# Hybrid block on one core: the hand-over from the mixer to the feed forward with its steps on VectorE in another order

## Chip, core and metric

The kernel runs on one core of a Trainium2 chip. The metric is the device time of one execution in microseconds (us). All tensors are float32. The five engines of the core each run their own queue of instructions in order: TensorE (PE: matmuls, with weight loads shown as PEld), VectorE (DVE), ScalarE (ACT), GpSimd (POOL) and SyncE (SP, which here only issues loads). They wait for each other through semaphores.

## What is computed

The reference is one block of a network on 512 tokens of 1024 features. The part that matters here, cut down:

```python
    # h, conv_out, ssm_out: norm, one large projection, a convolution branch and a state-space branch
    mixed = (g_conv * conv_out + g_ssm * ssm_out) @ w_out[i]
    x = x + rms_norm(mixed, mix_post_g[i])
    h = rms_norm(x, ffn_pre_g[i])
    gt, up = jnp.split(h @ w_gate_up[i], 2, axis=-1)       # 2 x 2816 columns
    f = (jax.nn.silu(gt) * up) @ w_down[i]
    x = x + rms_norm(f, ffn_post_g[i])
```

The hand-over is everything between the product with `w_out` and the product with `w_gate_up`: a norm, a residual sum, a second norm, and the transposition of `h` into the form in which the feed forward multiplies it.

## The kernel before

Each float32 product is made of three matmuls in a reduced form: an operand is split into a high part (a cast on ScalarE) and a low part (source minus high part), and `mm3` (L184 to L189) adds high x high, low x high and high x low. The low part is a subtraction on VectorE, or, for some weights, the negated high part written by ScalarE to which a load issued from POOL adds the weight from memory: an **adding load** (`accum_op=ALU.add`). `halve` (L927) makes the parts of a gate/up block, and `ADD_LO` (L78) names the units whose first block gets its low part by an adding load.

**Token tiles.** The product with `w_out` is made for four tiles of 128 tokens, t = 0 to 3, in `tm_step`. After each, `residual(t)` (L991) norms the result: the squares are summed on ScalarE (`mean_sq`), VectorE multiplies by the gain (`mg`, L1000), `factor` adds the two halves of the sum on VectorE (`pm`, L873) and raises them to -1/2 on POOL (`rs`, L874), VectorE adds the scaled result to x (`xr`, L1006). A second `mean_sq` and `factor` (`rs_b`) follow, and VectorE writes the diagonal matrix `dg` (L1010). `transposed(t)` (L1014) multiplies `xr` by `dg` on PE, which transposes and scales at once (tile `ptr`, L1023); the two halves of the result are scaled by the gain of the second norm into `xg`, the first half on VectorE (L1030), the second in four pieces on ScalarE (L1035).

**Halves.** The feed forward multiplies by Winograd's form of Strassen's scheme: seven products of halves instead of eight. The moving operands are b11 and b21 (from tiles 0 and 2), b22 and the sums t1 to t4 (from all tiles); for the second half of the tokens they are complete only after tile 3. `sums` and `rest` make them (L1060, L1066), each in a high and a low part.

**Units.** The 5632 columns of `w_gate_up` are cut into 22 units of 256, u = 0 to 21, gate and up in turn. A unit has two raw blocks of 128 x 1024 with the parts a11, a12 and a21, a22. `prep_a` makes the forms of a11 and a12; `prep_s` (L949) makes the sums s1 to s4 on VectorE (L956 to L961) and their forms (tiles `whi_g`/`wlo_g`, `chi_g`/`clo_g`, `dhi`/`dlo`, all at L930 and L935). A unit's seven products, 12 matmuls of 256 columns each, have names in the code:

- `first(u)`: a11 b11 into X and a12 b21 into Y, in one bank for the first four units;
- `begin(u)`: ScalarE copies X (L1118) and VectorE adds Y (L1107); this has to be done before X is used again;
- `x2(u)`: s2 t2 added into X; `v1(u)`: s1 t1; `x3(u)`: s3 t3; `v2(u)`: s4 b22; `x4(u)`: a22 t4 into X. After x2, v1 and x3 ScalarE or VectorE take the result over before the next product adds to the same bank.

The first four units overlap the hand-over in an order written out by hand. Before tile 3 is transposed PE makes `first(0)`, `first(1)`, `first(2)`; after it `first(3)` and then

```python
    start = {0: "v0 x0 v1 w0 y0", 1: "x1 w1 z0 y1", 2: "x2 v2 z1 y2", 3: "x3 v3 z2 w2 y3"}
    step = {"v": v1, "x": x2, "w": v2, "y": x3, "z": x4}
```

where the figure is the unit. From unit 4 on a loop makes them in a regular order.

The order of the instructions on an engine is decided before the run: the framework places each one by its estimate and by the order of the program's text, and `not_before` (L179) adds an order without a wait on data. `hold` is a pair of instructions: while it is set, forms and sums of weights are not placed ahead of them on ScalarE and VectorE. Raw blocks are loaded from SP into five shared buffers (`w_raw`, L142), so a load waits until the block that held its buffer has been split.

Of the kernel before, what the change touches and what calls it, by code (L numbers as in the profile page):

```python
# [10 lines left out]
F32 = mybir.dt.float32  # L11
# [66 lines left out]
ADD_LO = (2, 3) + tuple(range(7, FF // P, 2))  # L78
# [46 lines left out]
def block_kernel(ctx: ExitStack, tc: tile.TileContext, x, xT, x0, prm, hp, gp, w, out):  # L125
# [743 lines left out]
    def factor(ss, tag):  # L869

        rs = sm.tile([P, 1], F32, tag="rs1", bufs=2, name=f"rs_{tag}")
        m = sm.tile([P, 1], F32, tag="pm1", bufs=2, name=f"pm_{tag}")
        mark["pm"] = dve.tensor_scalar(out=m, in0=ss[0], scalar1=ss[1], scalar2=RMS_EPS, op0=ALU.add, op1=ALU.add)  # L873
        pool.tensor_tensor(out=rs, in0=m, in1=neg_half[:, :1], op=ALU.pow)  # L874
        return rs
# [72 lines left out]

    def prep_s(u):  # L949

        if u >= NF or (u, "s1") in forms:
            return
        ra, rb_ = g_raw(u, 0), g_raw(u, 1)
        (a11, a12), (a21, a22) = [(r[:, :T], r[:, T:]) for r in (ra, rb_)]
        s1_ = w2.tile([P, T], F32, tag="s1", bufs=2, name=f"s1_{u}")
        sum_ = dve.tensor_tensor(out=s1_, in0=a21, in1=a22, op=ALU.add)  # L956
        if hold:
            not_before(sum_, hold[1])
        dve.tensor_tensor(out=a21, in0=a11, in1=a21, op=ALU.add)
        dve.tensor_tensor(out=a11, in0=s1_, in1=a11, op=ALU.add)  # L960
        dve.tensor_tensor(out=a12, in0=a11, in1=a12, op=ALU.add)  # L961

        def s1_halves():
            halve(("s1",), u, s1_, [w2.tile([P, T], F32R, tag=tg, bufs=2, name=f"{tg}_{u}") for tg in ("dhi", "dlo")])

        def halves():
            halve(("s2", "s4"), u, ra, pair_of_tiles())
            if u != 1:
                s1_halves()
            halve(("s3", "a22"), u, rb_, pair_of_tiles())  # L970

        if u == 1:
            s1_halves()
        if u > 1:
            halves()
        return halves
# [14 lines left out]
    def residual(t, ps):  # L991
# [6 lines left out]
        for n, c in enumerate(cols2):  # L998
            ss.append(mean_sq(ps[n], pbp, f"a{t}", n))
            m = dve.tensor_tensor(out=mg[:, c], in0=ps[n], in1=gpost0[:, c], op=ALU.mult)  # L1000
        if t == 3:
            hold += [mark["sq"], m]
        rs = factor(ss, f"a{t}")
        ss = []
        for n, c in enumerate(cols2):
            dve.scalar_tensor_tensor(out=xr[:, c], in0=mg[:, c], scalar=rs, in1=xr[:, c], op0=ALU.mult, op1=ALU.add)  # L1006
            ss.append(mean_sq(xr[:, c], pbp, f"b{t}", n))
        rs = factor(ss, f"b{t}")
# [5 lines left out]
    def transposed(t):  # L1014
# [4 lines left out]
        for n in range(2):  # L1019
# [9 lines left out]
            if n == 0:  # L1029
                dve.tensor_tensor(  # L1030
# [49 lines left out]
    for t, k in steps:  # L1080
        (mh, ml), tok = mt[t // 2], slice(t % 2 * P, (t % 2 + 1) * P)
        tm_step(ps, t, k, NK, mh[:, k, tok], ml[:, k, tok], split[wo0 + k])
        if k == NK - 1:
            residual(t, ps[t])
            if t == 2:
                others()
# [5 lines left out]
        if (t, k) == (2, 5):  # L1092
            sums, others = transposed(1)
            sums()
        if (t, k) in ((3, 1), (3, 2)):
            prep_a(k + 1)
        if (t, k) == (3, 4):
# [13 lines left out]
    def begin(u):  # L1111

        f, e = u // 2, u % 2
        if e == 0:
# [19 lines left out]
    hold[1] = mark["pm"]  # L1134
    mark["chain"] = True
    for u in range(3):
        first(u)
        if u == 0:
            halves = prep_s(1)
# [3 lines left out]
    more_raw.append(h2e)  # L1143
    begin(0)
    sums()
    rest()
    hold[:] = mark["t3"]
# [11 lines left out]

    def x2(u):  # L1160
# [5 lines left out]
    def v1(u):  # L1166
        if u < EARLY_U:
            V[u] = bank(f"v{u}")[:, :HB]
        product(V[u], u, "s1", "t1", True)
        act.copy((D_[u][1] if u in D_ else begin(u)[1])[:, c2], V[u])  # L1170

    def x3(u):
        f, e = u // 2, u % 2
        d = D_[u][1][:, c2]
# [4 lines left out]
        else:  # L1179
            gated_by(d, d, sg[f][1][:, c2])  # L1180

    def v2(u):
# [6 lines left out]
        else:  # L1189
            dve.tensor_tensor(out=d, in0=d, in1=sg[f][0], op=ALU.mult)  # L1190

    def x4(u):
# [5 lines left out]
        else:  # L1198
            gated_by(d, X[u], sg[f][1][:, c1])
# [301 lines left out]
```

## Time and profile before

| | before |
|---|---|
| runs | 1029.85, 1036.62, 1037.15 us; median 1036.62 |
| profiled execution | 1036.17 us, of which the span is 1034.4 us |
| PE busy | 1024.2 us (99%), granted clock 0.998 on average |
| VectorE busy | 814.3 us (79%) |
| ScalarE busy | 609.0 us (59%) |
| POOL busy | 96.4 us (9%) |
| memory traffic | 150.82 MB, mean 146 GB/s |

In a row of the timeline stand the start and the duration in us, the engine, the line, the operation, the output and the inputs by their names in the program, the shape, and in brackets the idle time of the engine just before with what ended it. All times count from the start of the span. Token tile 3 leaves PE near 698 us, its transposition stands at 706.6, and unit 4 begins at 738.9.

### The profile page before, as it was taken

The page shows a single profiled execution, that of the slowest core. Times are in us where ns is not written, and L with a number is a line of the kernel's source. Part 1 is how long each engine was busy: PE and PEld are TensorE (multiplying, and loading weights), DVE is VectorE, ACT ScalarE, POOL GpSimd, SP SyncE. Part 2 cuts the span into 40 slices and gives each one's busy share as a digit, 9 for nine tenths or more (in the row PEclk, how much of TensorE's full clock was granted, in tenths as well). Part 3 has the DMA queues.
Part 4 walks back from the last instruction along what each step waited for, and adds up shares of the span by engine and source line. Part 5 has one row for each costly group of instructions (what it writes and reads, how often), then busy time and mean ns, then how long its engine had stood idle before and what let it go on. Part 6 is the DMA issues. An engine that isn't in the chain of part 4 may idle for free.

```text
span 1034.4 us, 15686 instructions
## 1 busy us (share of the span) xinstructions
PE 1024.2 (99%) x6089; PEld 890.9 (86%) x6089; DVE 814.3 (79%) x1184; ACT 609.0 (59%) x1032; POOL 96.4 (9%) x122
## 2 busy tenths in 40 slices
PE   9999999999999999999999999999999999999997
PEld 7898889888888888888888888889999999998885
DVE  7899976959594979398976455579997788799874
ACT  7655776575748464844532673366665565568552
POOL 0101101110111011101100000010000000001000
PEclk9999999999999999999999999999999999999999
DMA  8567634655546454644452223433565345469622
GB/s 298 156 164 213 165 81 140 184 157 148 135 131 163 124 157 128 163 122 122 110 133 84 82 85 99 183 105 121 167 184 157 105 143 146 123 197 278 214 82 82
DMA packets 42458, 150.82 MB, mean 146 GB/s; under 512 B 4880, under 2 KB 5904, under 8 KB 41360
## 3 DMA queue, kind: packets, MB, share of 16 engines
q1 hardware_dynamic: 30672, 104.66, 29.9%
q0 software_dynamic: 9504, 38.80, 19.0%
q10 hardware_dynamic: 2208, 6.36, 1.8%
q8 instruction: 48, 0.79, 0.3%
q14 instruction: 26, 0.21, 0.1%
HBM read 145.54 MB, written 4.26 MB: 145 GB/s over the span
## 4 chain that ended last, share of the span: by engine, by line
PE 93%; DVE 3%; ACT 2%; issue 1%; DMA 0%; POOL 0%; SPq 0%; ACTq 0%; POOLq 0%; DVEq 0%
PE xy L187 4%; PE xy L186 4%; PE xy L188 4%; PE pz L187 3%; PE pz L188 3%; PE pz L186 3%; PE pso L186 3%; PE pso L187 3%; PE pso L188 3%; PE px L188 3%; PE px L187 3%; PE px L186 3%; PE yv L187 2%; PE yv L188 2%; PE yv L186 2%; PE yd L636 2%
## 5 line engine op out<-in xcount | busy, mean ns | idle before, releaser
L152 ACT CAST whi<-raw 128x1024 fp32r<-128x1024 f32 (+2 forms) x116 | 115.0, 1003 | 157.3 <-PE pso L187 37.5
L444 DVE SCALAR_TENSOR_TENSOR a<-v,prm_t,a 128x511 f32<-128x511 f32 (+15 forms) x240 | 179.8, 752 | 16.1 <-ACT a L441 13.8
L158 DVE TENSOR_TENSOR wlo<-raw,whi 128x1024 fp32r<-128x1024 f32 (+2 forms) x76 | 85.8, 1134 | 42.8 <-ACT whi L152 42.1
L156 POOL DMA_DIRECT2D wlo<-in_w x40 | 35.7, 893 | 353.5 <-ACT wlo L155 120.9
L188 PE MATMUL pz<-whi,hlo 128*128 128x512 f32 (+2 forms) x160 | 56.3, 352 | 0.0
L187 PE MATMUL pz<-wlo,hhi 128*128 128x512 f32 (+2 forms) x160 | 56.1, 351 | 0.0
L186 PE MATMUL pz<-whi,hhi 128*128 128x512 f32 (+2 forms) x160 | 55.4, 353 | 0.0
L186 PE MATMUL px<-hhi,whi 128*128 128x512 f32 x128 | 50.2, 392 | 0.0
L186 PE MATMUL pso<-yh,whi 128*128 128x512 f32 x128 | 50.0, 393 | 0.0
L188 PE MATMUL px<-hhi,wlo 128*128 128x512 f32 x128 | 49.8, 389 | 0.0
L187 PE MATMUL px<-hlo,whi 128*128 128x512 f32 x128 | 49.8, 389 | 0.0
L187 PE MATMUL pso<-yl,whi 128*128 128x512 f32 x128 | 49.7, 390 | 0.0
L188 PE MATMUL pso<-yh,wlo 128*128 128x512 f32 x128 | 49.7, 389 | 0.0
L930 ACT CAST whi_g<-raw 128x1024 fp32r<-128x1024 f32 x40 | 41.3, 1053 | 13.7 <-PE yv L187 8.6
L528 DVE SCALAR_TENSOR_TENSOR x<-px,prm_t,x 128x511 f32<-128x511 f32 (+2 forms) x48 | 34.7, 741 | 13.8 <-ACT x L526 13.8
L935 DVE TENSOR_TENSOR wlo_g<-raw,whi_g 128x1024 fp32r<-128x1024 f32 x34 | 41.1, 1218 | 5.1 <-ACT whi_g L930 4.7
L155 ACT ACTIVATE wlo<-whi 128x1024 fp32r<-128x1024 f32 x40 | 42.2, 1055 | 0.3
L426 ACT ACTIVATE L<-L,nacs 128x128 f32<-128x128 f32 x128 | 38.8, 389 | 0.5 <-POOL L L419 0.4
L186 PEld LDWEIGHTS pz<-whi,hhi 128*128 128x128 f32 x160 | 30.2, 189 | 3.9
L187 PEld LDWEIGHTS pz<-wlo,hhi 128*128 128x128 f32 x160 | 30.2, 188 | 3.8
L188 PEld LDWEIGHTS pz<-whi,hlo 128*128 128x128 f32 x160 | 30.1, 188 | 3.7
L930 ACT CAST chi_g<-raw 128x1024 fp32r<-128x1024 f32 x24 | 24.8, 1050 | 11.4 <-PE yv L187 5.1
(656 smaller groups left out, 3344.8 us busy)
## 6 DMA issues: line engine op xcount, KB each, us to landing
raw<-in_w SPq DMA_DIRECT2D x186, 512.0 KB, 4.5
wlo<-in_w POOLq DMA_DIRECT2D x40, 512.0 KB, 6.8
L<-scr POOLq DMA_DIRECT2D x8, 1024.0 KB, 7.1
wlo_g<-in_w POOLq DMA_DIRECT2D x11, 512.0 KB, 7.1
clo_g<-in_w POOLq DMA_DIRECT2D x7, 512.0 KB, 5.3
xr<-in_x ACTq DMA_DIRECT2D x4, 512.0 KB, 4.7
x2d<-xr ACTq DMA_DIRECT2D x4, 512.0 KB, 2.9
xres<-x2d SPq DMA_DIRECT2D x4, 512.0 KB, 3.7
```

The costliest lines, as they stand in the source:

```text
L152: act.copy(hi[:, c], src[:, c])
L155: act.activation(lo[:, c], hi[:, c].bitcast(F32), AF.Copy, scale=-1.0)
L156: mark["lo"] = pool.dma_start(lo[:, c], w[n][:, c].bitcast(F32R), accum_op=ALU.add)
L158: mark["wlo"] = dve.tensor_tensor(out=lo[:, c], in0=src[:, c], in1=hi[:, c].bitcast(F32), op=ALU.subtract)
L186: mark["pe"] = pe.matmul(ps, lh, rh, start=start, stop=False, skip_group_check=more)
L187: pe.matmul(ps, lh, rl, start=False, stop=False, skip_group_check=more)
L188: mark["pe3"] = pe.matmul(ps, ll, rh, start=False, stop=stop, skip_group_check=more)
L426: act.activation(L[:, h, c, :], L[:, h, c, :], AF.Exp, bias=nacs[:, c, HG * g + h : HG * g + h + 1])
L444: return dve.scalar_tensor_tensor(out=va[j][:, d:], in0=vs[j][:, : T - d], scalar=col("dw_w", j * KC + KC - 1 - d), in1=va[j][:, d:], op0= ...
L528: dve.scalar_tensor_tensor(out=a[:, d:], in0=ps[:, : T - d], scalar=col("ssm_w", i * KS + KS - 1 - d), in1=a[:, d:], op0=ALU.mult, op1=ALU ...
L930: a_ = act.copy(hi, src)
L935: d_ = dve.tensor_tensor(out=lo, in0=src, in1=hi.bitcast(F32), op=ALU.subtract)
```

## The change

1. `transposed(2)` scales both halves of the third tile on VectorE.
2. `hold` now ends, for the last tile, with the residual sum `xr` instead of `mg`; for unit 0 it is moved on to `dg` while its blocks are split, and it is set to `pm` later.
3. For unit 1 the block sum s1 = a21 + a22 is made by loads: `load_s1` brings a21 from SP, `add_s1` adds a22 from POOL, placed not before the power of the third tile. a21 + a11 is then rebuilt as a difference.
4. `ADD_LO` names unit 4 too: the low part of its a11 and a12 comes by an adding load.
5. The `sums` of tile 1 and of tile 3 are called at other places, `begin(1)` is called before the splitting of unit 1, and gets a tile `d1` of its own in place of half of `f32`, which does not exist yet at that point. Its results go to `f32` through `f_out`.
6. For units 2 and on, the first block sum of `prep_s` is held behind t4.

```diff
@@ -75,7 +75,7 @@
 EARLY_U = 4
 DMA_EVERY = 2
 DMA_FROM = 8
-ADD_LO = (2, 3) + tuple(range(7, FF // P, 2))
+ADD_LO = (2, 3, 4) + tuple(range(7, FF // P, 2))
 GU_AHEAD = 5
 MOV_AT = 192
 S_AHEAD = 5
@@ -871,7 +871,7 @@
         rs = sm.tile([P, 1], F32, tag="rs1", bufs=2, name=f"rs_{tag}")
         m = sm.tile([P, 1], F32, tag="pm1", bufs=2, name=f"pm_{tag}")
         mark["pm"] = dve.tensor_scalar(out=m, in0=ss[0], scalar1=ss[1], scalar2=RMS_EPS, op0=ALU.add, op1=ALU.add)
-        pool.tensor_tensor(out=rs, in0=m, in1=neg_half[:, :1], op=ALU.pow)
+        mark["pow"] = pool.tensor_tensor(out=rs, in0=m, in1=neg_half[:, :1], op=ALU.pow)
         return rs
 
     def scale_of(srcs, pool_, tag):
@@ -946,18 +946,34 @@
             again = w[seq[("gu", 2 * u)]] if u in ADD_LO else None
             halve(("a11", "a12"), u, g_raw(u, 0), room or pair_of_tiles(), again)
 
+    s1s = {}
+
+    def load_s1(u):
+
+        s1s[u] = w2.tile([P, T], F32, tag="s1", bufs=2, name=f"s1_{u}")
+        nc.sync.dma_start(s1s[u], w[seq["gu", 2 * u + 1]][:, :T])
+
+    def add_s1(u):
+
+        return pool.dma_start(s1s[u], w[seq["gu", 2 * u + 1]][:, T:], accum_op=ALU.add)
+
     def prep_s(u):
 
         if u >= NF or (u, "s1") in forms:
             return
         ra, rb_ = g_raw(u, 0), g_raw(u, 1)
         (a11, a12), (a21, a22) = [(r[:, :T], r[:, T:]) for r in (ra, rb_)]
-        s1_ = w2.tile([P, T], F32, tag="s1", bufs=2, name=f"s1_{u}")
-        sum_ = dve.tensor_tensor(out=s1_, in0=a21, in1=a22, op=ALU.add)
+        if u in s1s:
+            s1_ = s1s[u]
+        else:
+            s1_ = w2.tile([P, T], F32, tag="s1", bufs=2, name=f"s1_{u}")
+            sum_ = dve.tensor_tensor(out=s1_, in0=a21, in1=a22, op=ALU.add)
+            if u > 1:
+                not_before(sum_, mark["t4"][1])
+            dve.tensor_tensor(out=a21, in0=a11, in1=a21, op=ALU.add)
+        sum_ = dve.tensor_tensor(out=a11, in0=s1_, in1=a11, op=ALU.add)
         if hold:
             not_before(sum_, hold[1])
-        dve.tensor_tensor(out=a21, in0=a11, in1=a21, op=ALU.add)
-        dve.tensor_tensor(out=a11, in0=s1_, in1=a11, op=ALU.add)
         dve.tensor_tensor(out=a12, in0=a11, in1=a12, op=ALU.add)
 
         def s1_halves():
@@ -967,6 +983,10 @@
             halve(("s2", "s4"), u, ra, pair_of_tiles())
             if u != 1:
                 s1_halves()
+            if u == 0:
+                hold[1] = mark["dg"]
+            if u == 1:
+                not_before(dve.tensor_tensor(out=a21, in0=a11, in1=a22, op=ALU.subtract), hold[1])
             halve(("s3", "a22"), u, rb_, pair_of_tiles())
 
         if u == 1:
@@ -997,14 +1017,15 @@
         ss = []
         for n, c in enumerate(cols2):
             ss.append(mean_sq(ps[n], pbp, f"a{t}", n))
-            m = dve.tensor_tensor(out=mg[:, c], in0=ps[n], in1=gpost0[:, c], op=ALU.mult)
-        if t == 3:
-            hold += [mark["sq"], m]
+            dve.tensor_tensor(out=mg[:, c], in0=ps[n], in1=gpost0[:, c], op=ALU.mult)
+        first_sq = mark["sq"]
         rs = factor(ss, f"a{t}")
         ss = []
         for n, c in enumerate(cols2):
-            dve.scalar_tensor_tensor(out=xr[:, c], in0=mg[:, c], scalar=rs, in1=xr[:, c], op0=ALU.mult, op1=ALU.add)
+            m = dve.scalar_tensor_tensor(out=xr[:, c], in0=mg[:, c], scalar=rs, in1=xr[:, c], op0=ALU.mult, op1=ALU.add)
             ss.append(mean_sq(xr[:, c], pbp, f"b{t}", n))
+        if t == 3:
+            hold += [first_sq, m]
         rs = factor(ss, f"b{t}")
         dg = pbp.tile([P, P], F32, tag="dg", name=f"dg{t}")
         mark["dg"] = dve.tensor_scalar(out=dg, in0=ident, scalar1=rs, scalar2=None, op0=ALU.mult)
@@ -1026,8 +1047,8 @@
                     mark["pe3"] = m
             tg = dict(tag=f"xg{t}{n}", bufs=1) if t % 2 == 0 else dict(tag=f"xg{n}", bufs=1)
             xg.append(pmp.tile([P, KB, P], F32, name=f"xg{t}_{n}", **tg))
-            if n == 0:
-                dve.tensor_tensor(
+            if n == 0 or t == 2:
+                mark["xg"] = dve.tensor_tensor(
                     out=xg[n], in0=pt, in1=b3(prm_t[:, FPG + KB * n : FPG + KB * n + KB], P), op=ALU.mult
                 )
             else:
@@ -1083,6 +1104,7 @@
         if k == NK - 1:
             residual(t, ps[t])
             if t == 2:
+                sums()
                 others()
         if (t, k) == (2, 1):
             transposed(0)
@@ -1091,9 +1113,12 @@
                 prep_a(u, [m[:, u] for m in first_room])
         if (t, k) == (2, 5):
             sums, others = transposed(1)
-            sums()
         if (t, k) in ((3, 1), (3, 2)):
             prep_a(k + 1)
+        if (t, k) == (3, 2):
+            load_s1(1)
+        if (t, k) == (3, 6):
+            not_before(add_s1(1), mark["pow"])
         if (t, k) == (3, 4):
             halves = prep_s(0)
         if (t, k) == (3, 5):
@@ -1111,7 +1136,10 @@
     def begin(u):
 
         f, e = u // 2, u % 2
-        if e == 0:
+        if u == 1:
+            d1 = h2e.tile([P, T], F32, tag="d1", bufs=1, name="d1")
+            D_[u] = [d1, None]
+        elif e == 0:
             sg[f] = D_[u] = [h2e.tile([P, T], F32, tag=f"sg{i}", bufs=2, name=f"sg{f}_{i}") for i in range(2)]
         else:
             D_[u] = [f32[:, 2 * f + i, :] for i in range(2)]
@@ -1131,19 +1159,20 @@
         product(Y[u], u, "a12", "b21", u >= EARLY_U)
 
     halves()
-    hold[1] = mark["pm"]
     mark["chain"] = True
     for u in range(3):
         first(u)
         if u == 0:
+            hold[1] = mark["pm"]
             halves = prep_s(1)
     sums, rest = transposed(3)
     pb.close()
     h2e = h2.enter_context(tc.tile_pool(name="h2e", bufs=2))
     more_raw.append(h2e)
+    sums()
     begin(0)
-    sums()
     rest()
+    begin(1)
     hold[:] = mark["t3"]
     halves()
     hold[:] = mark["t4"]
@@ -1157,6 +1186,9 @@
     fp = ctx.enter_context(tc.tile_pool(name="f", bufs=1, side="right"))
     f32 = fp.tile([P, NF, T], F32, name="f32")
 
+    def f_out(u, i):
+        return f32[:, u - 1 + i, :] if u % 2 else D_[u][i]
+
     def x2(u):
         if u not in D_:
             begin(u)
@@ -1167,17 +1199,19 @@
         if u < EARLY_U:
             V[u] = bank(f"v{u}")[:, :HB]
         product(V[u], u, "s1", "t1", True)
+        if u == 1:
+            D_[u][1] = f32[:, 1, :]
         act.copy((D_[u][1] if u in D_ else begin(u)[1])[:, c2], V[u])
 
     def x3(u):
         f, e = u // 2, u % 2
-        d = D_[u][1][:, c2]
+        d, to = D_[u][1][:, c2], f_out(u, 1)[:, c2]
         product(X[u], u, "s3", "t3", False)
         add(d, X[u])
         if e == 0:
             act.activation(d, d, AF.Silu, scale=-1.0)
         else:
-            gated_by(d, d, sg[f][1][:, c2])
+            gated_by(to, d, sg[f][1][:, c2])
 
     def v2(u):
         f, e = u // 2, u % 2
@@ -1187,7 +1221,7 @@
         if e == 0:
             act.activation(d, d, AF.Silu)
         else:
-            dve.tensor_tensor(out=d, in0=d, in1=sg[f][0], op=ALU.mult)
+            dve.tensor_tensor(out=f_out(u, 0), in0=d, in1=sg[f][0], op=ALU.mult)
 
     def x4(u):
         f, e = u // 2, u % 2
@@ -1196,7 +1230,7 @@
         if e == 0:
             act.activation(d, X[u], AF.Silu, scale=-1.0)
         else:
-            gated_by(d, X[u], sg[f][1][:, c1])
+            gated_by(f_out(u, 1)[:, c1], X[u], sg[f][1][:, c1])
 
     def gated_by(out_, src, by):
         dve.scalar_tensor_tensor(out=out_, in0=src, scalar=-1.0, in1=by, op0=ALU.mult, op1=ALU.mult)
```

## Prediction

> **What bounds the kernel now.** I read the page first: busy shares, then the chain that ended last.
>
> ```profile
> span 1034.4 us, 15686 instructions
> ...
> PE 1024.2 (99%) x6089; PEld 890.9 (86%) x6089; DVE 814.3 (79%) x1184; ACT 609.0 (59%) x1032; POOL 96.4 (9%) x122
> ...
> PE 93%; DVE 3%; ACT 2%; issue 1%; DMA 0%; POOL 0%; SPq 0%; ACTq 0%; POOLq 0%; DVEq 0%
> ```
>
> TensorE (PE) is busy 99% of the span, so a change of order on VectorE (DVE) can only win back moments in which PE waits. Next comes the timeline of PE around the hand-over. Two rows stand for each place where two starts lie further apart than one matmul; the bracket is the idle time that the view itself notes.
>
> ```profile
> 697.83 0.28 PE L186 MATMUL xy<-b11h,a01h 128*128 128x256 f32 x1
> 698.18 0.39 PE L187 MATMUL xy<-b11l,a01h 128*128 128x256 f32 x1
> ...
> 703.63 0.28 PE L186 MATMUL xy<-b11h,whi_g 128*128 128x256 f32 x1
> ...
> 704.99 0.28 PE L186 MATMUL xy<-b21h,whi_g 128*128 128x256 f32 x1
> ...
> 706.23 0.28 PE L188 MATMUL xy<-b21h,wlo_g 128*128 128x256 f32 x1
> 706.59 2.02 PE L1023 MATMUL ptr<-dg,xr 128*128 128x128 f32 x16
> ...
> 711.19 0.28 PE L186 MATMUL v<-t1h,dhi 128*128 128x256 f32 x1
> 711.88 0.38 PE L187 MATMUL v<-t1l,dhi 128*128 128x256 f32 x1 [0.42 <-DVE t1l L1041]
> ...
> 718.58 0.28 PE L188 MATMUL xy<-t3h,clo_g 128*128 128x256 f32 x1
> 719.28 0.39 PE L186 MATMUL xy<-t2h,chi_g 128*128 128x256 f32 x1 [0.42 <-DVE f L1107]
> ...
> 722.01 0.28 PE L188 MATMUL v<-b22h,clo_g 128*128 128x256 f32 x1
> 722.35 0.39 PE L186 MATMUL xy<-t4h,chi_g 128*128 128x256 f32 x1
> ...
> 725.28 0.28 PE L186 MATMUL xy<-t2h,whi_g 128*128 128x256 f32 x1
> ...
> 728.19 0.28 PE L188 MATMUL v<-t1h,dlo 128*128 128x256 f32 x1
> 728.89 0.38 PE L186 MATMUL xy<-t4h,chi_g 128*128 128x256 f32 x1 [0.42 <-DVE f L1107]
> ...
> 738.89 0.28 PE L186 MATMUL xy<-b11h,whi_g 128*128 128x256 f32 x1
> ...
> 740.30 0.28 PE L186 MATMUL yv<-b21h,whi_g 128*128 128x256 f32 x1
> ```
>
> From 703.63 to 704.99 lie the twelve matmuls of one product, 0.113 us each. Taking 0.113 (0.12 at the last place) from each gap leaves PE's waits: 0.24 at 698.18, 0.25 at 706.59, 0.58 at 711.88, 0.59 at 719.28, 0.23 at 722.35, 0.58 at 728.89, together 2.47 us. **That is all this change can win from waits: 0.24%.** No later wait of this stage shows. What ends the waits is VectorE, and the table of windows, here from 718 to 740, says how full it is:
>
> ```profile
> 718.00:740.00 22.00, 21.09 (x174) 20.35 (x173) 22.00 (x37) 15.01 (x25) 0.00 (x0) 1.00 0.57 190
> ```
>
> After the length come the busy times of PE, weight loads, VectorE and ScalarE: VectorE is busy 22.00 of 22.00 us. So in this stretch an instruction placed later in its queue comes later by the full length of what was put ahead of it. Also to be seen in the PE rows: the product from 738.89 to 740.30 took 1.41 us, that from 703.63 to 704.99 1.36, though the granted clock (the 1.00 behind POOL's share) was full.
>
> **The change part by part.** I keep one account: how early or late PE reaches a named matmul, against the rows above.
>
> ```profile
> 697.43 0.69 DVE L1041 TENSOR_TENSOR b11l<-xg,b11h 128x512 fp32r<-128x512 f32 x1 [1.89 <-ACT b11h L1040]
> ...
> 700.20 1.22 DVE L935 TENSOR_TENSOR wlo_g<-raw,whi_g 128x1024 fp32r<-128x1024 f32 x1
> 701.89 1.41 DVE L1006 SCALAR_TENSOR_TENSOR xr<-mg,rs_a,xr 128x512 f32<-128x512 f32 x2 [0.46 <-POOL rs_a L874]
> ...
> 710.20 0.69 DVE L1062 TENSOR_TENSOR t<-t,xg 128x512 f32<-128x512 f32 x1
> ...
> 713.55 0.68 DVE L1070 TENSOR_TENSOR t<-t,xg 128x512 f32<-128x512 f32 x1
> 714.15 0.41 DVE L1107 TENSOR_TENSOR sg<-xy,sg 128x256 f32<-128x256 f32 x1
> 714.49 0.68 DVE L1041 TENSOR_TENSOR t3l<-t,t3h 128x512 fp32r<-128x512 f32 x1
> ...
> 717.07 1.22 DVE L935 TENSOR_TENSOR clo_g<-raw,chi_g 128x1024 fp32r<-128x1024 f32 x1
> 718.21 0.68 DVE L956 TENSOR_TENSOR s<-raw 128x512 f32<-128x512 f32 x1
> ```
> ```profile
> 691.60 0.34 ACTq L995 DMA_DIRECT2D xr<-in_x  x1
> ...
> 695.75 1.14 ACT L1035 ACTIVATE xg<-ptr,prm_t 128x128 f32<-128x128 f32 x4 [2.17 <-PE ptr L1023]
> ...
> 708.65 1.15 ACT L1035 ACTIVATE xg<-ptr,prm_t 128x128 f32<-128x128 f32 x4 [2.23 <-PE ptr L1023]
> ```
> ```profile
> 675.55 0.54 POOL L874 TENSOR_TENSOR rs_a<-pm_a,neg_half 128x1 f32<-128x1 f32 x1 [4.45 <-DVE pm_a L873]
> ...
> 700.23 1.63 POOL L874 TENSOR_TENSOR rs_a<-pm_a,neg_half 128x1 f32<-128x1 f32 x1 [5.35 <-DVE pm_a L873]
> ```
>
> From start to start VectorE takes 0.60 us for a step of 512 columns (713.55 to 714.15), 0.34 for 256 (714.15 to 714.49), 1.14 for 1024 (717.07 to 718.21).
>
> *Third tile scaled on VectorE.* ScalarE's four scalings (1.14) stand ahead of its cast b11h. Without them that cast starts about 1.1 us sooner, VectorE pays one step of 0.60 while it would be waiting (the 1.89), and b11l ends near 697.0. The wait at 698.18 goes: **-0.24**. Were the cover gone, the step would cost at most its 0.60.
>
> *xr ahead of wlo_g.* The power rs_a took 1.63 us while wlo_g ran beside it, 0.54 where nothing did. Now VectorE goes on to xr, so xr starts near 700.2 and not at 701.89; its load, issued at 691.60 and landed 7.2 us later (row below), is there by 698.8, so the adding half of unit 1's sum may slow it by 1.4 us at no cost. dg, the last thing before the transposing matmuls, comes near 705 rather than 706.21, and PE asks for it at 706.10: **-0.25**, covered by about 1 us. [...]
>
> *The block sum of unit 1 by an adding load.* It takes one 0.60 step from VectorE; the subtract that rebuilds a21 replaces an add of the same size. Its first half is queued on SP right behind the loads for units 0 to 3 and waits for nothing late; the adding half goes to POOL's queue after rs_b of the third tile, about 692.6, and is wanted at 704. No row shows an adding load of 256 KB; bounded by nothing and by the 7.6 us of one of 512 KB (row below) it lands by 700.2. Ahead of rs_a in that queue, it has 7 us to issue: **0**; if it were late, rs_a and the adding load of unit 3 behind it would be.
>
> *What follows for t1l and unit 1.* The transposing matmuls end 0.49 earlier, ScalarE's xg (708.65 to 709.80) does too, and t2 (the row at 710.20) starts near 709.35, t1l ends near 710.6; PE wants it at 710.8: **-0.58**. The start of unit 1 now stands ahead of t3l, near 713.5, where before it was the f of 718.81: **-0.59**. PE is now 1.66 ahead and reaches the t4 product of unit 0 at about 720.46.
>
> *That product's wait.* It needs the add after x3(0) (now L1132). Ahead of it from 709.35 stand 13 steps of 512, 3 of 256 and 2 of 1024: 7.8 + 1.0 + 2.3 = 11.1. It starts at 720.45 and ends at 720.9: PE waits 0.44 instead of 0.23 and is 1.45 ahead.
>
> *The start of unit 2: the step that decides.* In the old order its add (the sg at 714.15) stands before t3l. In the order of the changed program it stands after the steps of units 1, 2 and 3, directly behind the add after x3(1). PE can't begin x2(2) (725.28 before) without it, since that product accumulates into the same bank. Ahead of it from 709.35: 20 steps of 512, 6 of 256, 4 of 1024, 12.0 + 2.0 + 4.6 = 18.6 us, so it starts at 727.95 and ends near 728.4. PE would be there at 725.28 - 1.45 = 723.83: **a new wait of 4.57**, and x2(2) starts 3.12 late. The later wait (0.58 at 728.89) falls away, since its add now comes before unit 2's; restarting after one wait instead of another is even. **Net +2.5 us.**
>
> [...]
>
> *Low part of unit 4 by an adding load.* VectorE loses a step of 1.14 after the late add; ScalarE gains a negation of about the length of a cast.
>
> ```profile
> 728.78 2.95 ACT L930 CAST whi_g<-raw 128x1024 fp32r<-128x1024 f32 x3
> ```
> ```profile
> wlo_g<-in_w POOLq DMA_DIRECT2D x2, 512.0 KB, 7.6
> ...
> xr<-in_x ACTq DMA_DIRECT2D x1, 512.0 KB, 7.2
> ...
> clo_g<-in_w POOLq DMA_DIRECT2D x1, 512.0 KB, 5.1
> ```
>
> ScalarE's three casts (2.95) now follow unit 3's last sum on VectorE, which ends near 727.0 by the count above; with the negation that is 731. Issued then and landed after 5.1 to 7.6 us, the load is there by 738.6; PE wants it at 738.89 + 2.5 = 741.4. **0**, with 3 us of cover that exists only because PE is late. The separate tile d1 for unit 1 and the changed outputs move no work.
>
> Sum: 1036.17 (the profiled execution's own time; its span is 1034.4, 1.8 lie around it) + 2.5 = **1038.7 us**. The median of the three runs, 1036.62, is 0.45 above that execution.
>
> Bounds: if t2 starts 1.5 us sooner or later steps are that much shorter, +1.0; if VectorE waits 2 us for a block of unit 2 or 3 among those steps (loads behind its own late casts), +4.5. So 1037.2 to 1040.7 for this case.
>
> **The rivals.** *A, faster: the gains stand and unit 2 is not late.* Then waits of 1.66 + 0.58 go, 0.2 come back, and unit 4's load, wanted near 737, costs 0 to 1.5: 1034.1 to 1035.6. For it: PE's waits all point at VectorE's late steps. Against it: the place of the add in the queue and 18.6 us of quoted durations. It decides if the add of unit 2 ends before 724.
>
> *B, the pace.* Of 154 products some 137 come after x2(2); at 1.36 instead of 1.41 us each that is 6.9 us. The runs before, 1029.85 against 1036.62 and 1037.15, differ by 6.8 to 7.3, which is what one run at the faster pace would give (my inference). The pace was fast after the waits at 698, 711 and 719, which ended on b11, t1 and t2, and slow from 722 on. If the new wait, which ends on t2, sets the fast pace, the time is 1038.7 - 6.9 plus up to 1 us of waits that a faster PE meets: 1031.8 to 1032.8. Against it: at that pace PE meets VectorE again at the next t4 product.
>
> *C, slower by more: unit 4's adding load comes late.* It shares the DMA engines with loads that SP issues behind the same VectorE steps. Its place is the third matmul of unit 4's first product, which needs the low part near 741.6; each microsecond that it lands later costs one, so it decides from 10.6 us of landing time on. At twice the slower row, 15.2, it lands at 746.2: +4.6, 1043.3. Against it: 7.6 was measured with three other transfers under way, and clo_g, issued at a time when VectorE was full, took 5.1. [...]
>
> **How the numbers follow.** Main case 0.58, B 0.22, A 0.12, C 0.08. The predicted time is 1038.7. The range of 1031.0 to 1041.5 holds main, A and B; main alone is 1037.2 to 1040.7. One per cent, about what a measurement of this kernel can tell from no change, is 10.4 us: main, A and B lie inside; only A with the fast pace (near 1027) touches the lower bound, only C beyond its price the upper. Faster 0.04, same 0.91, slower 0.05.
>
> **What would show it.** Right: no bracket at v<-t1l; the L1132 add on sg for unit 2 near 728 with wlo_g steps ahead of it; PE idle some 4.5 us before xy<-t2h,whi_g, released by that add; first product of unit 4 near 741.4; later products of 1.41 us. Wrong: PE's idle time there under 1 us (A), products of 1.36 after it (B), or idle time before the products of unit 4 (C).

## The result and the profile after

Over 20 runs of each, the changed kernel has a median of **1035.17 us** against 1030.66 us: 1.0038 of the time before, 95% interval 1.0019 to 1.0056. It is slower by 4.5 us by the medians, where the prediction had 1038.7 against a base of 1036.6, that is 2.1 to 2.5 us slower. The first execution of it, 1465.56 us at a granted clock of 0.654, is left out of the times; the profile below is of an execution of 1034.72 us (span 1032.9, granted clock 0.997).

The times of both kernels lie in two groups:

| 20 runs each | lower group (mean) | upper group (mean) |
|---|---|---|
| before | 14 runs, 1029.7 to 1031.2 (1030.39) | 6 runs, 1036.2 to 1037.3 (1036.91) |
| changed | 15 runs, 1033.5 to 1036.3 (1034.80) | 4 runs, 1041.0 to 1041.9 (1041.38) |

Group against group the change costs 4.4 and 4.5 us. In the lower group of the changed kernel ten times have a granted clock of 0.997 (mean 1034.36) and five have 0.994 to 0.996 (mean 1035.66). The profile that the prediction used (1036.17) was one of the upper group. A second profile of the kernel before, of 1029.82 us, is of the lower one. TensorE in one and the same stretch, first in the prediction's profile, then in the second one (us of the stretch, PE's busy time and matmuls, granted clock, DMA share, GB/s):

```profile
750.00:900.00 150.00, 150.00 (x1276) 1.00 0.49 138
```
```profile
750.00:900.00 150.00, 150.00 (x1326) 1.00 0.53 150
```

PE is busy all the time in both, at the same granted clock, and does 1276 matmuls in one and 1326 in the other: 0.1176 against 0.1131 us each. The groups are these two paces (the eight profiles in which such a stretch was counted bear it out, see the last section), and what follows compares lower group with lower group.

The hand-over in the second profile of before (timeline of PE: start, us, idle time before it and what ended it in brackets):

```profile
697.88 0.28 PE L186 MATMUL xy<-b11h,a01h 128*128 128x256 f32 x1
698.23 0.39 PE L187 MATMUL xy<-b11l,a01h 128*128 128x256 f32 x1
...
725.23 0.28 PE L186 MATMUL xy<-t2h,whi_g 128*128 128x256 f32 x1
...
728.93 0.38 PE L186 MATMUL xy<-t4h,chi_g 128*128 128x256 f32 x1 [0.50 <-DVE f L1107]
```

And in the changed kernel, same view:

```profile
698.78 0.28 PE L186 MATMUL xy<-b11h,a01h 128*128 128x256 f32 x1
698.90 0.28 PE L187 MATMUL xy<-b11l,a01h 128*128 128x256 f32 x1
...
721.18 0.28 PE L188 MATMUL v<-b22h,clo_g 128*128 128x256 f32 x1
722.04 0.38 PE L186 MATMUL xy<-t4h,chi_g 128*128 128x256 f32 x1 [0.58 <-DVE sg L1132]
...
724.77 0.28 PE L188 MATMUL xy<-t3h,clo_g 128*128 128x256 f32 x1
729.61 0.36 PE L186 MATMUL xy<-t2h,whi_g 128*128 128x256 f32 x1 [4.57 <-DVE sg L1132]
...
730.26 0.32 PE L188 MATMUL xy<-t2h,wlo_g 128*128 128x256 f32 x1
730.38 0.42 PE L186 MATMUL xy<-t2h,whi_g 128*128 128x256 f32 x1
730.59 0.42 PE L187 MATMUL xy<-t2l,whi_g 128*128 128x256 f32 x1
...
733.91 0.28 PE L188 MATMUL v<-t1h,dlo 128*128 128x256 f32 x1
734.03 0.28 PE L186 MATMUL xy<-t4h,chi_g 128*128 128x256 f32 x1
...
743.78 0.28 PE L188 MATMUL xy<-b11h,wlo_g 128*128 128x256 f32 x1
```

The 4.57 stands where the prediction put it. It is the idle time of the bracket, counted from the modelled end of the matmul before; start to start less one matmul, as the prediction counts, the wait is 4.73. What it did not have stands behind it: from 730.38 the matmuls start 0.21 us apart instead of 0.11. The windows of the same profile (us, then busy time and instructions of PE, PEld, DVE, ACT and POOL, the granted clock, DMA share, GB/s) show why:

```profile
724.90:729.60 4.70, 0.15 (x2) 0.02 (x1) 4.70 (x9) 1.89 (x4) 0.00 (x0) 1.00 0.66 219
729.60:730.30 0.70, 0.69 (x6) 0.70 (x7) 0.70 (x1) 0.70 (x2) 0.00 (x0) 1.00 0.14 35
730.30:733.70 3.40, 3.40 (x19) 3.40 (x18) 3.37 (x6) 2.19 (x3) 0.89 (x1) 0.51 0.47 164
```

For 3.4 us PE was granted half its clock. Counted from the first b11 matmul of each execution (which lies between 697.8 and 699.3 in the profiles, also among kernels with the same program up to there):

| | before, 1029.82 | changed, 1034.72 | difference |
|---|---|---|---|
| x2(2) starts | 27.35 | 30.83 | +3.48 |
| second t4 product starts | 31.05 | 35.25 | +4.20 |
| end of the span | 330.12 | 334.12 | +4.00 |

All of it is there by 734. VectorE's steps and POOL's in the changed kernel:

```profile
710.42 0.69 DVE L1083 TENSOR_TENSOR t<-t,xg 128x512 f32<-128x512 f32 x1 [0.65 <-ACT xg L1056]
711.03 0.68 DVE L1062 TENSOR_TENSOR t1l<-t,t1h 128x512 fp32r<-128x512 f32 x1
...
724.04 2.35 DVE L935 TENSOR_TENSOR wlo_g<-raw,whi_g 128x1024 fp32r<-128x1024 f32 x2
...
729.06 0.41 DVE L1132 TENSOR_TENSOR sg<-xy,sg 128x256 f32<-128x256 f32 x1
```
```profile
700.76 0.56 POOL L874 TENSOR_TENSOR rs_a<-pm_a,neg_half 128x1 f32<-128x1 f32 x1 [4.96 <-DVE pm_a L873]
...
732.67 0.89 POOL L933 DMA_DIRECT2D wlo_g<-in_w  x1 [27.03 <-ACT sg L1196]
```
```profile
wlo_g<-in_w POOLq DMA_DIRECT2D x1, 512.0 KB, 10.5
```

The add of unit 2 starts 18.6 us behind t's second step (710.42 to 729.06), the figure of the prediction. Unit 4's adding load, issued at 732.67, lands 10.5 us later at 743.2; PE asks for it at 743.78.

### The profile page after: what moved, and what is told of

It reads as the page before. It is cut to its first block, busy times and chain, and to the rows that moved or that the text cites. A ratio compares the mean times of both kernels' runs of the same rounds, so it can differ in the third digit from the quotient of the medians.

```text
span 1463.8 us, 15702 instructions
## 1 busy us (share of the span) xinstructions
PE 1453.2 (99%) x6089; PEld 1069.1 (73%) x6089; DVE 826.5 (56%) x1183; ACT 614.1 (42%) x1029; POOL 96.9 (7%) x124
## 4 chain that ended last, share of the span: by engine, by line
PE 99%; DVE 1%; DMA 0%; issue 0%; ACT 0%; DVEq 0%; POOLq 0%; ACTq 0%
PE xy L186 4%; PE xy L187 4%; PE xy L188 4%; PE pz L187 3%; PE pz L186 3%; PE pz L188 3%; PE pso L186 3%; PE pso L188 3%; PE px L186 3%; PE px L187 3%; PE pso L187 3%; PE px L188 3%; PE yv L188 2%; PE yv L186 2%; PE yv L187 2%; PE yd L636 2%
## 5 line engine op out<-in xcount | busy, mean ns | idle before, releaser
L188 PE MATMUL pz<-whi,hlo 128*128 128x512 f32 (+2 forms) x160 | 71.8, 448 | 0.0
L187 PE MATMUL pz<-wlo,hhi 128*128 128x512 f32 (+2 forms) x160 | 71.7, 448 | 0.0
L186 PE MATMUL pz<-whi,hhi 128*128 128x512 f32 (+2 forms) x160 | 70.9, 449 | 0.0
L186 PE MATMUL px<-hhi,whi 128*128 128x512 f32 x128 | 65.4, 511 | 0.0
L186 PE MATMUL pso<-yh,whi 128*128 128x512 f32 x128 | 64.9, 510 | 0.0
L188 PE MATMUL px<-hhi,wlo 128*128 128x512 f32 x128 | 64.9, 507 | 0.0
L187 PE MATMUL px<-hlo,whi 128*128 128x512 f32 x128 | 64.9, 507 | 0.0
L187 PE MATMUL pso<-yl,whi 128*128 128x512 f32 x128 | 64.8, 507 | 0.0
L188 PE MATMUL pso<-yh,wlo 128*128 128x512 f32 x128 | 64.6, 506 | 0.0
L709 DVE TENSOR_TENSOR so<-pso,so 128x512 f32<-128x512 f32 x24 | 16.6, 691 | 50.7 <-PE pso L188 50.7
```

Source lines behind the costliest of these rows:

```text
L186: mark["pe"] = pe.matmul(ps, lh, rh, start=start, stop=False, skip_group_check=more)
L187: pe.matmul(ps, lh, rl, start=False, stop=False, skip_group_check=more)
L188: mark["pe3"] = pe.matmul(ps, ll, rh, start=False, stop=stop, skip_group_check=more)
```

## The experiments

"Lower" and "upper" are the two groups of times of each run.

**The changed kernel and the one before, again.**

> The changed kernel as it is, for a profile at the full clock (the one at hand was taken at a granted clock of 0.654, where TensorE is slow against VectorE). Its 20 times so far lie in two groups, 1033.5 to 1036.3 (15) and 1041.0 to 1041.9 (4); those of the kernel before as well, 1029.7 to 1031.2 (15) and 1036.2 to 1037.3 (5). Group against group the change costs 4 to 4.5 us. Theory L (late add of unit 2): VectorE's add on sg for unit 2 (L1132) ends near 728 with two wlo_g steps ahead of it, PE idles 4 to 6 us before xy<-t2h,whi_g and is released by that add; the times repeat the two groups. Rival U (adding load of unit 4): PE idles under 1 us there, and 3 to 5 us ahead of the third matmul of unit 4's first product near 740, released by a DMA. Rival D (spread): no single wait of over 2 us between 690 and 760; the 4 us are made of several small ones or of longer matmuls.

Lower 1034.4 to 1036.0 (5), upper 1041.03 (1); ratio 1.0055 (1.0039 to 1.0071). Theory L holds for place and size of the wait, and U and D fall. The half clock was in no theory. (The kernel before had 14 and 6 times in the two groups, as in the table above, not 15 and 5.)

> The kernel before as it is, for a second profile. If the two groups of times are two paces of TensorE, a run near 1030.4 shows products of 12 matmuls at 1.36 us to the end of the feed forward's first part where the profile of 1036.17 shows 1.41 us from 722 to 919; a run near 1036.9 shows 1.41 us again. If the groups have another cause, both profiles have the same spacing of matmuls and differ in waits.

1029.82, at the spacing of 0.113 us: the two groups are two paces.

**Unit 2 begun early.**

```diff
     rest()
     begin(1)
+    begin(2)
```

> The changed kernel with one line more: unit 2 is begun right behind unit 1, so that its add stands in VectorE's queue ahead of the low parts of units 1, 2 and 3 and not behind them. Theory L: the wait before xy<-t2h,whi_g (4 to 6 us) goes, and nothing of the same size takes its place at once; the time falls by 3 to 5 us against the changed kernel, to 1029.5 to 1031.5 in the lower group, about level with the kernel before or 1 us under it. Rival U: no change in the time (within 0.5 us of 1034.6). Rival D: a fall of under 1.5 us.

Lower 1037.39 (4), upper 1042.5 (2): slower by 2.1 us than the changed kernel's 1035.31, measured beside it. The expected number was wrong, yet the wait before x2(2) is gone. PE comes to unit 4 some 4.4 us sooner, counted from the first b11 matmul, and waits there (PE's timeline, then the DMA issues of 733 to 744):

```profile
738.72 0.28 PE L187 MATMUL xy<-b11l,whi_g 128*128 128x256 f32 x1
743.22 0.58 PE L188 MATMUL xy<-b11h,wlo_g 128*128 128x256 f32 x1 [4.23 <-DMA wlo_g<-in_w]
743.60 0.41 PE L186 MATMUL xy<-b11h,whi_g 128*128 128x256 f32 x1
```
```profile
raw<-in_w SPq DMA_DIRECT2D x4, 512.0 KB, 7.4
wlo_g<-in_w POOLq DMA_DIRECT2D x1, 512.0 KB, 9.7
```

It is the third matmul of unit 4's first product, where rival C had put it. The changed kernel hides this second late operand behind the first.

**Unit 4's low part on VectorE again** (ADD_LO without 4).

> The changed kernel with unit 4's low part computed on VectorE again, as before the change (ADD_LO without 4). Theory L: nothing gained, 0 to 1 us slower than the changed kernel, since VectorE has one step of 1.14 us more behind the late add. Rival U: faster by 3 to 5 us. Rival D: under 1.5 us either way.

Lower 1035.19 (4) against 1035.31, upper 1041.61 (2): nothing, since the load is just in time while unit 2 is late. The same wait was followed by more half clock in this execution (PE's timeline, two windows of all engines):

```profile
729.17 0.55 PE L186 MATMUL xy<-t2h,whi_g 128*128 128x256 f32 x1 [4.58 <-DVE sg L1132]
```
```profile
724.30:729.10 4.80, 0.29 (x3) 0.09 (x1) 4.80 (x9) 1.98 (x4) 0.00 (x0) 0.77 0.61 203
...
733.10:735.10 2.00, 2.00 (x17) 2.00 (x16) 1.81 (x3) 0.80 (x2) 0.00 (x0) 0.85 0.88 281
```

Between these two windows the clock is 0.50 throughout, so half the clock lasted from 726.9 to 733.7, 6.8 us, of which 2.3 lie inside the wait. x2(2) and the product behind it took 4.93 us (729.17 to 734.10) where the changed kernel's profile has 4.42. Over the whole execution the granted clock is 0.994 here (1041.22 us) and 0.997 there (1034.72 us), so the five slower times in the lower group of the changed kernel may be executions of this kind; no profile of one was taken.

**Unit 4's adding load alone, on the kernel before** (ADD_LO with 4).

> The kernel before with one edit of the change alone: unit 4's low part by an adding load. Theory A: the load is issued near 732, lands 9 to 11 us later among the loads that SP issues in the same 3 us, and PE asks for it at 738.8: a wait of 3 to 4.5 us at the third matmul of unit 4's first product, with half the granted clock behind it if it is over 3 us; lower group 1033.5 to 1036.5. Rival (the prediction's bounds of 5.1 to 7.6 us of landing hold where the late add is away): landed by 739.6, wait under 1 us, 1030 to 1031.3.

Lower 1037.77 (5), upper 1042.22 (2); the lower is 7.1 us above the 1030.63 of the kernel before, measured beside it, and more than expected (PE's timeline, DMA issues of 734 to 746):

```profile
744.73 0.58 PE L188 MATMUL xy<-b11h,wlo_g 128*128 128x256 f32 x1 [4.69 <-DMA wlo_g<-in_w]
```
```profile
raw<-in_w SPq DMA_DIRECT2D x5, 512.0 KB, 5.9
wlo_g<-in_w POOLq DMA_DIRECT2D x1, 512.0 KB, 10.0
```

A wait of 4.7 us, and a granted clock of 0.995 over the whole execution, against 0.998 in the second profile of before: by the author's estimate, from these two means, some 6 us at half the clock. By itself this edit costs more than the whole change.

**Both late operands away.**

```diff
-ADD_LO = (2, 3, 4) + tuple(range(7, FF // P, 2))
+ADD_LO = (2, 3) + tuple(range(7, FF // P, 2))
...
     begin(1)
+    begin(2)
```

> The changed kernel with unit 2 begun right behind unit 1 and unit 4's low part on VectorE. With unit 2 begun early alone, PE waited 4.2 us at the third matmul of unit 4's first product for the adding load and then ran at half the granted clock for some 3 us. Theory A (two waits, the adding load hidden behind the late add): without both, PE reaches unit 4 some 40.4 us after its first b11 matmul (before: 40.7, changed: 44.8) and meets no wait there; lower group of times 1029.7 to 1030.5, level with the kernel before. Rival B (VectorE is full, so any order gives the time back later): a wait of 2 us or more moves to another product behind unit 4, lower group 1031.5 to 1035.

Lower 1030.82 (3), upper 1036.62 (8): level with before (1030.63 and 1036.78) group by group, so theory A holds, though the lower group lies 0.3 us above its range. PE's time from the first b11 matmul to unit 4 is 40.75 us, a part of it at the slower pace. The rest of the change's gain went into one place: the t4 product of unit 0 now waits 1.68 us (start to start, less one matmul) for the add after x3(0), and the next one 0.98 (PE's timeline; the granted clock of the whole execution is 0.999, the matmuls from 723.39 on start 0.116 us apart). The median, 1036.28, is worse only because 8 of 11 times are in the upper group.

```profile
723.17 0.38 PE L186 MATMUL xy<-t4h,chi_g 128*128 128x256 f32 x1 [1.52 <-DVE sg L1132]
```

**The tile d1 and the early start of unit 1 undone, unit 4's load away.**

```diff
-        if u == 1:
-            d1 = h2e.tile([P, T], F32, tag="d1", bufs=1, name="d1")
-            D_[u] = [d1, None]
-        elif e == 0:
+        if e == 0:
...
     rest()
-    begin(1)
```

> The changed kernel with the separate tile d1 and the early start of unit 1 undone and unit 4's low part on VectorE; the third tile's scaling, the earlier xr, the sums ahead of the start of unit 0 and unit 1's block sum by a load stay. Theory A: unit 2's add is back in the slot behind t's last step (near 714), since unit 1's start no longer takes that slot; no wait of over 1.5 us before x2(2), granted clock 1.00 throughout; lower group 1029.5 to 1030.5. Rival B: unit 1's start now comes late by the same amount (its add stands behind the first step of unit 2's sums) and PE waits over 2 us before its t2 product: 1032 to 1034.

Lower 1030.37 (6), upper 1036.80 (5); before 1030.63 and 1036.78. VectorE's timeline and PE's:

```profile
713.65 0.68 DVE L1091 TENSOR_TENSOR t<-t,xg 128x512 f32<-128x512 f32 x1
714.25 0.42 DVE L1132 TENSOR_TENSOR sg<-xy,sg 128x256 f32<-128x256 f32 x1
```
```profile
719.74 0.38 PE L186 MATMUL xy<-t2h,chi_g 128*128 128x256 f32 x1 [1.17 <-DVE f L1132]
```

Unit 2's add is back at 714.25, directly behind t's last step. So the early start of unit 1 is the edit that moved it (the kernel above with unit 4's low part on VectorE differs from this one in it and its tile alone, and has 1035.19): it took the slot in which unit 2's add used to stand. Unit 1 pays now (1.17), as rival B had it, but for 1.2 us and not 2.

**A shorter wait.** Unit 2 begun later in the program, its add held behind unit 2's second wlo_g; ADD_LO without 4.

```diff
+            if u == 2:
+                mark["low"] = low
...
+        if u == 0:
+            begin(2)
         prep_s(max(u + 1, 3))
...
-        add(D_[u][0][:, c1], Y[u])
+        a_ = add(D_[u][0][:, c1], Y[u])
+        if u == 2:
+            not_before(a_, mark["low"])
```

> The changed kernel with unit 4's low part on VectorE and unit 2's add placed right behind unit 2's own two wlo_g steps, three steps and an add sooner than in the changed kernel: PE's wait before xy<-t2h,whi_g should be about 2.0 us and not 4.6. Theory G (a wait of over some 3 us costs twice: the wait, and about 1.7 us at half the granted clock behind it): the matmuls behind the wait keep a spacing of 0.11 us and the granted clock stays at 1.00, so the time falls by 2.7 + 1.7 = 4.4 us against the changed kernel without unit 4's load (1035.2), to 1030.5 to 1031.5 in the lower group. Rival W (half the clock follows any wait at this place, or the cost of the restart does not depend on the length of the wait): the products behind it take 2.0 and 2.4 us again and the time falls by 2.7 us, to 1032.0 to 1033.0.

Lower 1031.75 (4), upper 1036.69 (7); the lower is 3.4 us under the 1035.19 of the kernel with the full wait: between the two theories. The profile decides (PE's timeline, a window):

```profile
724.58 0.28 PE L188 MATMUL xy<-t3h,clo_g 128*128 128x256 f32 x1
726.68 0.36 PE L186 MATMUL xy<-t2h,whi_g 128*128 128x256 f32 x1 [1.83 <-DVE sg L1135]
```
```profile
727.20:730.60 3.40, 3.40 (x18) 3.40 (x17) 2.46 (x6) 1.40 (x3) 0.00 (x0) 0.50 0.64 249
```

Half the clock for 3.4 us again, behind 1.83 us of idle time: G's length of some 3 us is wrong. Waits of 1.52 and 1.17 us in the two kernels above had no half clock behind them, by the granted clocks of 0.999 and 0.998 over those two executions. The granted clocks of this kernel's other executions say more. The profiled one, with 3.4 us at half clock, has 0.997 over the whole; the four lower times have 0.996 or 0.997, and six of the seven upper ones have 0.998 or 0.999, as kernels without half clock do. Those six (mean 1036.62) are 5.0 us under the upper group of the kernel with the full wait, where the lower four gained 3.4. So the same wait seems to pass with the half clock or without it, and the difference of 1.6 us is what it costs; this is read from the mean clocks, without a profile of one of the six.

**The same wait, filled.** ADD_LO without 4, unit 2's add as late as in the change.

```diff
+        if u == 2:
+            V[u] = bank(f"v{u}")[:, :HB]
+            for _ in range(20):
+                m = pe.matmul(V[u][:, :P], ident, ident, start=True, stop=True)
...
         product(X[u], u, "s2", "t2", False)
```

> The changed kernel with unit 4's low part on VectorE, unit 2's add left as late as it is, and 20 matmuls of 128 columns (the identity, into the bank that unit 2's next product overwrites) ahead of xy<-t2h,whi_g: at 0.2125 us each (8 took 1.70) they fill 4.25 of the 4.7 us in which PE has nothing to do. Nothing that the output needs is done sooner. Theory G (half the granted clock follows when PE has been idle for about half of some 3.4 us): granted clock 1.00 behind the wait, spacing of 0.113 to 0.118 us, x2(2) and the product behind it take 2.8 us together instead of 4.9; the time falls by 1.7 to 2.1 us against the changed kernel without unit 4's load, to 1033.0 to 1033.8 in the lower group, 1039.5 to 1040.2 in the upper. Rival N (the slow matmuls belong to the late operands, VectorE and the loads being as busy as they are there, and not to PE's idle time): the two products take 4.9 us again, no change (1034.9 to 1035.5). Rival M (the extra matmuls themselves hold up what follows): slower by up to 0.5 us.

One group, 1032.5 to 1034.5 (12, mean 1033.28), every one at a granted clock of 0.998 or 0.999: 1.9 us faster than 1035.19, by work that nothing needs (PE's timeline, a window):

```profile
725.39 4.63 PE L1198 MATMUL v<-ident 128*128 128x128 f32 x40
730.12 0.36 PE L186 MATMUL xy<-t2h,whi_g 128*128 128x256 f32 x1
```
```profile
730.10:733.50 3.40, 3.38 (x29) 3.40 (x30) 3.40 (x4) 2.32 (x4) 0.00 (x0) 1.00 0.39 101
```

The operand is as late as ever, VectorE as full, the clock stays at 1.00: the half clock follows PE's idle time and not the late operand or VectorE's work. That much of theory G is shown, its figure of half of some 3.4 us is not; N and M fall.

**Unit 4's cast called earlier.** Unit 2 begun early, unit 4's adding load kept.

```diff
+        if u == 0:
+            prep_a(4)
         prep_s(max(u + 1, 3))
```

> The changed kernel with unit 2 begun right behind unit 1, and unit 4's cast called before unit 3's sums, so that it stands ahead of unit 3's casts on ScalarE and its adding load can be issued near 727 instead of 733. Theory A (the load was late because of its issue, behind unit 3's last sums on VectorE): landed by 737.5 even if it takes 10.5 us again, wanted at 738.9; no wait at the third matmul of unit 4's first product; lower group 1029.7 to 1031.2, some 7 us under the same kernel with the late issue. Rival B (the transfer itself is slow whenever it shares the DMA engines with the loads of SP's queue, and gets later as they do): it lands at 740 or later and PE waits over 1 us there; lower group 1032 or more.

Lower 1031.49 (5), upper 1036.17 (7): 5.9 and 6.3 us under the same kernel with the late cast. Issue and landing:

```profile
728.19 0.89 POOL L933 DMA_DIRECT2D wlo_g<-in_w  x1 [22.12 <-ACT sg L1232]
```
```profile
wlo_g<-in_w POOLq DMA_DIRECT2D x1, 512.0 KB, 5.6
```

It left 5 us sooner (733.43 there), took 5.6 us instead of 9.7 and landed at 733.8. Theory A holds, though the lower group lies 0.3 us above its range. The load was also quicker than it allowed for. What made it so is not shown: SP issued four loads from 727 to 735 here, and four from 733 to 744 in the kernel with the late cast.

**Unit 3's sums one unit later**, on top of that.

```diff
         if u == 0:
             prep_a(4)
-        prep_s(max(u + 1, 3))
+        else:
+            prep_s(3 if u == 1 else u + 1)
```

> As the kernel with the early cast of unit 4, with unit 3's sums called one unit later, so that the add after x3(1) stands ahead of most of them. Theory A (PE's wait of 0.98 us before the second t4 product comes from that order alone): the wait goes, x2(3) waits some 0.5 us for unit 3's low part instead, 0.3 to 0.6 us are gained against the kernel with the early cast. Rival B (VectorE's work up to unit 3 is the bound): the wait moves whole to x2(3), no gain within 0.2 us.

Lower 1030.41 (8), upper 1036.43 (4); before 1030.51 and 1037.44; ratio 0.9998 (0.9973 to 1.0023). The wait of 0.98 is gone and 0.77 stands at x2(3). Against the kernel with the early cast alone the lower group gained 1.1 us and the upper lost 0.3, so neither theory is decided. This is the best order found, and it does not beat the kernel before. That VectorE is the bound of this stretch, so that an order alone makes it no shorter, fits this but is argued, not shown.

**The pace.**

```diff
+        if u == 4:
+            for _ in range(8):
+                m = pe.matmul(X[u][:, :P], ident, ident, start=True, stop=True)
...
         product(X[u], u, "a11", "b11", True)
```

> The changed kernel with unit 2 begun early and unit 4's low part on VectorE (11 times: 3 at 1030.1 to 1031.2, 8 at 1036.2 to 1037.2), and in front of unit 4's first product 8 matmuls of 128 columns of the identity into that product's own bank, whose result the product overwrites; 0.8 to 0.9 us of extra work. In the nine profiles so far each stretch of 256-column matmuls between two restarts of PE runs wholly at one spacing, 0.113 or 0.118 us, and the stretch behind the 128-column transposing matmuls ran at 0.113 in all nine. Theory R (the spacing is settled at a restart, and 128-column matmuls ahead of it settle it at 0.113): nearly all times near 1031 to 1032, one group. Rival S (the spacing is a property of the execution, not of the restart): the two groups stay in about the same shares, 1031 to 1032 and 1037 to 1038, with products of 1.41 us behind the 8 matmuls in some.

Ten of 12 times at 1031.6 to 1034.2 (mean 1032.45), two at 1036.4 and 1037.3; without the 8 matmuls 3 of 11 were in the lower group. They took 1.70 us, twice the expected price:

```profile
739.04 1.95 PE L1160 MATMUL xy<-ident 128*128 128x128 f32 x16
740.74 0.37 PE L186 MATMUL xy<-b11h,whi_g 128*128 128x256 f32 x1
```

The median fell by 3.7 us with 1.7 us of work added. Theory R holds for most executions; the two that stayed slow are not explained.

## Why the prediction was right or wrong

**Third tile, xr, dg, t1l, start of unit 1: right.** At 698.90, at dg and at t1l there is no wait, the power took 0.56 us in its new place, where VectorE waits for it, and the first wait comes at the t4 product. The power of 0.54 us in the prediction's rows had a step of VectorE beside it too, for 0.46 us (xg, at 675.33), so these rows alone do not show what makes it 0.5 us or 1.6 long. What the wait at b11l was worth is not sure: behind it the stretch up to the transposes ran at 0.113 us in the prediction's profile (698.40 to 706.12), and without it the first matmuls of the changed kernel ran at 0.118 (698.78 to 699.25). Over the 72 of the stretch that would cost 0.3 us, as much as the wait (the author's estimate).

**Block sum by an adding load: right.** It was in time; VectorE goes on without a wait for it.

**The t4 product of unit 0: nearly.** 0.75 us start to start, less one matmul (722.04 less 721.18, less 0.11), where the working had 0.44.

**The start of unit 2: right.** 18.6 us from t's second step, a wait of 4.57 expected, and 4.73 by the same count (the 4.57 in the bracket counts otherwise, and agrees to the last place by luck); x2(2) came 3.48 us late where 3.12 was worked out.

**"Restarting after one wait instead of another is even": this step failed.** The wait at 728.89 went, as said, but what came in its place was 3.4 us at half the clock: x2(2) and the product behind it took 4.42 us (729.61 to 734.03) instead of 2 x 1.36, so 1.70 us more. Before, this stretch from x2(2) to the next t4 product took 3.70 us, so it is 0.72 longer where the working had it 0.58 shorter. With 3.48 that makes the 4.2 us. The kernel with the filled wait shows the price on its own: 1.9 us of time, a mean over executions that differ, by their granted clocks, in how long they ran at half. How much idle time brings it on is not known: 1.83 us were enough in one execution.

**Unit 4's adding load at nothing: right for the wrong reason.** It took 10.5 us, not 5.1 to 7.6, and was issued 1.7 us later than worked out (0.9 of it because the hand-over began later in this execution). It landed 0.6 us before PE asked, because PE was later still. The prediction did say that its cover exists only because PE is late, and rival C has the place and the time from which it decides (10.6, a hair above the 10.5); its price of one microsecond for each is too low, since half the clock follows (0.50 from 743.2 to 745.2 in the kernel with unit 2 begun early). Alone on the kernel before the load costs 7.1 us, with a wait of 4.69. The term that was mis-sized is the landing time: its rows were of other moments, with three other transfers under way by its own count, and here SP issued five loads from 731 to 744. What sets the landing time is not shown.

**The base, and rival B.** 1038.7 was summed from an execution at the slower pace. B's figures hold (137 products at 1.36 instead of 1.41 us, 6.9; the groups lie 6.5 us apart), and so does its guess about the three runs. But the pace is no effect of this change: 14 of 20 runs of before and 15 of the 19 used of the changed kernel are in the lower group. The sum should have been a difference, to be added to either group.

**A** fell with the 4.57. "Within 1%" was right.

## What to carry to other kernels

Before an add or a copy is moved forward, look at what stood in its slot: in a full, ordered queue the step that nobody placed is the one that is pushed out, here by 14 us (from 16.3 to 30.3 us behind the first b11 matmul). Price a wait of a tensor engine by what the clock does behind it, too (here 3.4 us at half behind 4.57 us of idle time), and fill it with matmuls, useless ones too, if it can't be removed (20 of them gained 1.9 us). And when two operands are late, the second hides behind the first: take the first away alone and the kernel can become slower, here by 2.1 us.

## What the runs showed of the hardware

- Half the granted clock for 3.4 us at PE's idle times of 4.57, 4.23 and 1.83 us, for 6.8 us at 4.58; none behind 1.52 and 1.17, by mean clocks of 0.999 and 0.998; none with the same late operand when other matmuls filled the wait (1.00).
- In the trace of the changed kernel's first execution the half clock lasted 3.413 us (1034.95 to 1038.36), and all changes of the granted clock in it, and in the prediction's profile, lie whole multiples of that apart: 302, 1 and 124 in the one, 300 in the other. The half clocks of 3.4 and 6.8 us in the hand-over are as long as one and two. So, by the author's estimate, it hangs on where a wait falls in these steps whether none, one or two of them pass at half the clock. How much of a step has to be idle was not measured.
- Two spacings of 256-column matmuls, 0.113 and 0.118 us, at a granted clock of 1.00. In the prediction's profile the spacing was 0.113 to 0.114 behind the waits at 698.18, 711.88 and 719.28, and 0.118 behind those at 722.35 and 728.89, from the last one on for 1619 matmuls. In eight profiles a stretch of 150 or 160 us behind 750 was counted: 0.118 in the four of the upper group, 0.113 in the three of the lower and in the kernel with the filled wait, whose 12 times are one group. Behind 128-column matmuls the spacing was 0.113 in the prediction's profile (708.58 to 711.07) and, from 750 on, in the kernels with the 8 and the 20 of them; but 2 of 12 times of the kernel with the 8 are in the upper group. What picks it is open.
- An adding load of 512 KB took 5.6 us where it was issued at 728.19, 9.7 where it was issued at 733.43, 10.5 at 732.67, and 10.0 alone on the kernel before.
